# Turning tiles by 16-bit transposing transfers in place of TensorE transposes, in a streaming-encoder block

## The chip, the cores and the metric

The kernel runs on one core of a Trainium2 chip. The metric is the device time of one execution in microseconds, as the median of several runs. A profiled execution gives the trace from which single durations are read.

## The reference

One layer of a hybrid encoder block on 256 tokens of 2048 features, in float32. Norms are RMS norms with a gain, and every branch is added to the residual `x`:

```
x += 1/2 * SwiGLU(norm(x))                      # d_ff = 5632: h @ w_up, silu(gate) * up, @ w_down
h = norm(x); proj = h @ w_in                    # HGRN2 q f i g | RG-LRU x gate | branch gates A B
y_A = HGRN2(q, f, i) (normed, * silu(g))        # chunked gated linear recurrence
y_B = RG-LRU(conv4(x_b)) * gelu(gate_b)         # associative scan
merged = sigmoid(gate_A) * (y_A @ w_a) + sigmoid(gate_B) * (y_B @ w_b)
x += merged @ w_out
x += CrossAttention(norm(x), norm(mem))         # 4 heads, 256 memory tokens
x += 1/2 * SwiGLU(norm(x))
out = norm(x)
```

## The kernel before

**Products.** All large products are made at float32 precision from two float32r parts: a raw tile `raw` is copied to a high part `h` on ScalarE (`split`, L155), and VectorE writes the low part `l = raw - h` (L156). A product is then three matmuls: h by high, h by low, l by high. Weights come as 128x2048 tiles (1 MB). `weights()` keeps two weight tiles prepared ahead of TensorE; the tiles of the high parts come from a pool of three, `hp`, those of the low parts from a pool of three, `lp`. SyncE issues the loads, GpSimd the accumulating loads (L274, L313) and the transfers that prepare sums of weights ahead (L212, L218). The feed-forwards combine weight blocks so that seven products replace eight; the sums that this needs are VectorE's work (L304 to L307, and `ready` ones that were prepared and stored earlier).

**Stages.** First feed-forward, input projection with the two recurrences beside it, gates, the branch products (`ab`), the output product (`out`), cross-attention (`q`, `k`, `mv`, scores, `o`), second feed-forward. Each feed-forward runs over 11 groups of 512 hidden features: eight weight tiles of `w_up` per group, and after a group some blocks of `w_down` of earlier groups (`ffn_order`).

**Turns.** The residual `xt[c]` (four tiles of 512 features), the merged branches and the gated activations are kept by tokens, 128 tokens on the partitions. A product needs them by features. `turned` (L496) and `turn` in `ffn` (L607) do this with TensorE: eight transposes of 128x128 float32 for one tile of 128x1024, into two PSUM banks. From PSUM, ScalarE copies the high part (`Operands.add` L396, `add_two` L407, `hidop` L611, `operand_pairs` L520) and VectorE writes the low part (L397, L408, L612).

A tile is turned after the next weight blocks have been issued, by lists of delayed calls: `late` in the stages, whose `flush` runs everything in it after the high parts of a product, and `late` in `ffn`, where a call waits for a number of ticks, one tick a weight tile:

```
late.append((4 if g else 2, lambda g=g, hid=(e0, e3): turn(g, hid)))
```

The order within each engine is then made by a list scheduler that follows the order of the program as far as operands and buffers allow. Each engine works through its instructions in order, so an instruction that waits holds up those behind it.

Of the kernel before, what the change touches and what calls it, by code (L numbers as in the profile page):

```python
# [8 lines left out]
F32 = mybir.dt.float32  # L9
F32R = mybir.dt.float32r  # L10
ACT = mybir.ActivationFunctionType
ALU = mybir.AluOpType

P = 128
# [80 lines left out]
def block_kernel(ctx: ExitStack, tc: tile.TileContext, xT, xin, memT, vec, gfin, bgate, lruw, wu1, wd1, win, wv,  # L95
# [265 lines left out]

    def flush(late):
        while late:
            late.pop(0)()

    def summed(acc, out=None, by=None):
# [9 lines left out]
    class Operands:  # L376
# [13 lines left out]
        def add(self, src, gain=None):  # L390
            t = self.new()
            if gain is None:
                act.activation(t[:, :T], src, ACT.Copy)
                dve.tensor_tensor(out=t[:, T:], in0=src, in1=t[:, :T].bitcast(F32), op=ALU.subtract)
            else:
                act.activation(t[:, :T], src, ACT.Copy, scale=gain)  # L396
                dve.scalar_tensor_tensor(out=t[:, T:], in0=src, scalar=gain, in1=t[:, :T].bitcast(F32),  # L397
                                         op0=ALU.mult, op1=ALU.subtract)
# [91 lines left out]
    def turned(tile, which=range(2)):  # L490
# [22 lines left out]
    def operand_pairs(src, gain, q, xg, out, every=False):  # L513


        for a in src:
            i = len(out)
            g = xg[:, i * 512:(i + 1) * 512]
            for z in range(2):
                act.activation(g[:, z * T:][:, :T], a[:, z * T:(z + 1) * T], ACT.Copy,  # L520
                               scale=col(gain, 4 * q + 2 * i + z))
            h, l = slot(F32R, "xh"), slot(F32R, "xl")
# [59 lines left out]
    }  # L582

    def ffn(name, pairs, sq, then, begin=(), sums=()):

# [7 lines left out]
        hids, accs = {}, {}  # L593
        late = []
        rstd = None
# [6 lines left out]
        def turn(g, hid):  # L602
            for y in range(2):
# [7 lines left out]
                act.activation(ov[:, :, 0], av, ACT.Copy)  # L611
# [11 lines left out]
        for at, e in enumerate(order):  # L623
# [3 lines left out]
            if kind != "down":  # L627
# [13 lines left out]
                if ends or last:  # L641
                    if ends or kind == "plain":
# [3 lines left out]
                        else:  # L646
                            ev = scoped["wide"].tile([P, 2048], F32, name="ev", tag="wide")
                            e0, e1, e2, e3 = (ev[:, i * 512:(i + 1) * 512] for i in range(4))
                        if rstd is None:
# [6 lines left out]
                if last:  # L656
# [3 lines left out]
                    else:  # L660
# [119 lines left out]
    def to_mix(c, t):  # L780
# [295 lines left out]
    def merge(c, accs):  # L1076
# [8 lines left out]
        def turn():  # L1085
            for acc in turned(m):
                merged.add_two(acc)

        late.append(turn)

    accs = []
    for g in range(8):
        accs.append([bank(), bank()])
        for kq in range(2):
            rows_product(accs[-1], ys.tiles[8 * (g % 2):], weights("ab", g, kq), 4 * kq, kq == 0, kq == 1)
            flush(late)
        if g % 2:
# [9 lines left out]
    for c in range(4):  # L1107
        accs = [bank(), bank()]
        for kq in range(4):
            rows_product(accs, merged.tiles, weights("out", c, kq), 4 * kq, kq == 0, kq == 3)  # L1110
            flush(late)
# [88 lines left out]
    pairs2, sums2, sq4 = [], [], TokenSquares()  # L1200

    def to_ffn(c):
        out = []
        sums2.append(operand_pairs(turned(xt[c]), "ffn2_norm", c, slot(name="xg"), out, every=True))
        pairs2.extend(out)
# [14 lines left out]
    for c in range(4):  # L1220
        accs = [bank(), bank()]
        for kq in range(4):
            rows_product(accs, os.tiles, weights("o", c, kq), 4 * kq, kq == 0, kq == 3)
            flush(late)
# [125 lines left out]
```

## Time and profile before

| | |
|---|---|
| median of 3 runs | 2417.07 us (2416.99 to 2417.82) |
| the profiled execution | 2418.76 us, of which the span of the trace is 2417.0 us |
| TensorE busy | 2405.1 us |
| VectorE busy | 2044.6 us |
| ScalarE busy | 1468.6 us |
| GpSimd busy | 102.3 us |
| moved by DMA | 684.33 MB, 283 GB/s over the span |

The trace lists each instruction with its line, engine, tiles written and read, start and duration. PE is TensorE (PEld its weight loads), DVE VectorE, ACT ScalarE, POOL GpSimd, SP SyncE; a q behind the name is the engine's queue, which issues transfers. Matmuls are pipelined: the duration of one overlaps the next, so that the distance between two starts is the time for which one occupies the engine. Groups show `out<-in` with the tiles' names, a count, busy microseconds, the mean duration in nanoseconds, and the engine's idle time just before, with what ended it.

### The profile page before, as it was taken

To read this page: it belongs to the slowest core of one execution; us is meant where nothing else is said; L and a number is where in the kernel's file an instruction comes from. 1 tells how busy PE (TensorE), PEld (TensorE's weight loads), DVE (VectorE), ACT (ScalarE), POOL (GpSimd) and SP (SyncE) were. 2 spreads that over 40 slices of the span, in tenths; PEclk is the share of its full clock that TensorE was granted. 3 is DMA by queue.
4 is the path that set the end of the run, shared out by engine and by line. 5 is a ranking of instruction groups with operands and counts; after the bars stand their busy time and mean duration, and the time that the engine had idled before them with its cause. 6 is when DMAs were issued, how large, how long until landed. Compare 5 with 4: busy or idle time off the path is not lost.

```text
span 2417.0 us, 30834 instructions
## 1 busy us (share of the span) xinstructions
PE 2405.1 (100%) x12116; PEld 2006.3 (83%) x12116; DVE 2044.6 (85%) x2275; ACT 1468.6 (61%) x1499; POOL 102.3 (4%) x166
## 2 busy tenths in 40 slices
PE   9999999999999999999999999999999999999998
PEld 8888888888888888888888888888888788888887
DVE  6999999999866878678876787777789999999995
ACT  8566777777654454476434555545676666666664
POOL 0000000000000000000000000000000000000000
PEclk9999999999999999999999999999999999999999
DMA  8578999999858776878989899876788877787773
GB/s 305 203 227 258 276 277 278 273 275 271 270 215 318 276 285 240 302 269 324 353 323 348 291 358 344 324 286 244 265 344 308 292 283 279 269 287 279 285 282 140
DMA packets 102386, 684.33 MB, mean 283 GB/s; under 512 B 11360, under 2 KB 11616, under 8 KB 29280
## 3 DMA queue, kind: packets, MB, share of 16 engines
q1 hardware_dynamic: 78192, 518.68, 57.5%
q0 software_dynamic: 23328, 162.54, 22.4%
q8 instruction: 95, 1.56, 0.2%
q10 hardware_dynamic: 720, 1.13, 0.1%
q14 instruction: 51, 0.42, 0.0%
HBM read 619.39 MB, written 62.91 MB: 282 GB/s over the span
## 4 chain that ended last, share of the span: by engine, by line
PE 97%; DVE 1%; ACT 1%; DMA 1%; issue 0%; ACTq 0%
PE acc L566 18%; PE acc L567 18%; PE acc L569 18%; PE acc L332 11%; PE acc L357 8%; PE acc L358 8%; PE acc L360 8%; PE acc L335 6%; PE acc L607 1%; PE acc L496 1%; ACT h L155 1%; DVE l L156 0%; PE acc L904 0%; DMA raw<-wd 0%; PE acc L1197 0%; PE acc L1151 0%
## 5 line engine op out<-in xcount | busy, mean ns | idle before, releaser
L155 ACT ACTIVATE h<-raw 128x2048 fp32r<-128x2048 f32 (+3 forms) x578 | 867.6, 1526 | 618.8 <-PE acc L358 209.5
L156 DVE TENSOR_TENSOR l<-raw,h 128x2048 fp32r<-128x2048 f32 (+2 forms) x406 | 833.8, 2056 | 209.3 <-ACT h L155 206.3
L566 PE MATMUL acc<-h,xh 128*128 128x512 f32 x1228 | 478.4, 392 | 0.5 <-ACT h L155 0.5
L567 PE MATMUL acc<-h,xl 128*128 128x512 f32 x1228 | 476.1, 390 | 0.0
L357 PE MATMUL acc<-h,ops 128*128 128x512 f32 x832 | 326.8, 393 | 0.0
L358 PE MATMUL acc<-h,ops 128*128 128x512 f32 x832 | 324.6, 390 | 0.0
L332 PE MATMUL acc<-ops,h 128*128 128x512 f32 x1152 | 278.0, 393 | 0.0
L566 PE MATMUL acc<-h,hidop 128*128 128x512 f32 x704 | 276.3, 392 | 1.5 <-ACT h L155 1.5
L566 PEld LDWEIGHTS acc<-h,xh 128*128 128x128 f32 x1228 | 230.5, 188 | 54.4 <-ACT h L155 6.2
L567 PE MATMUL acc<-h,hidop 128*128 128x512 f32 x704 | 274.4, 390 | 0.0
L567 PEld LDWEIGHTS acc<-h,xl 128*128 128x128 f32 x1228 | 230.6, 188 | 46.7
L332 PEld LDWEIGHTS acc<-ops,h 128*128 128x128 f32 x1152 | 211.6, 188 | 41.6
L156 DVE TENSOR_TENSOR tl<-raw,h 128x1024 fp32r<-128x1024 f32 x172 | 203.7, 1220 | 13.8 <-ACT h L155 13.3
L360 PE MATMUL acc<-l,ops 128*128 128x512 f32 x832 | 205.8, 389 | 0.0
L155 ACT ACTIVATE h<-td 128x1024 fp32r<-128x1024 f32 x140 | 146.6, 1055 | 82.6 <-DVE td L304 31.5
L569 PE MATMUL acc<-l,hidop 128*128 128x512 f32 x704 | 190.5, 389 | 0.0
L360 PEld LDWEIGHTS acc<-l,ops 128*128 128x128 f32 x832 | 156.2, 188 | 32.4
L357 PEld LDWEIGHTS acc<-h,ops 128*128 128x128 f32 x832 | 156.2, 188 | 32.3
L358 PEld LDWEIGHTS acc<-h,ops 128*128 128x128 f32 x832 | 156.3, 188 | 31.5
L569 PE MATMUL acc<-tl,xh 128*128 128x512 f32 x624 | 178.1, 392 | 0.1
L156 DVE TENSOR_TENSOR tl<-td,h 128x1024 fp32r<-128x1024 f32 x140 | 170.1, 1220 | 8.3 <-ACT h L155 7.4
L569 PE MATMUL acc<-l,xh 128*128 128x512 f32 x604 | 166.5, 390 | 0.0
(245 smaller groups left out, 2750.5 us busy)
## 6 DMA issues: line engine op xcount, KB each, us to landing
raw<-wu SPq DMA_DIRECT2D x114, 1024.0 KB, 6.3
raw<-wd SPq DMA_DIRECT2D x88, 1024.0 KB, 6.5
prep<-wu POOLq DMA_DIRECT2D x58, 1024.0 KB, 6.5
t<-prep POOLq DMA_DIRECT2D x58, 1024.0 KB, 5.7
raw<-t SPq DMA_DIRECT2D x58, 1024.0 KB, 7.1
raw<-wu SPq DMA_DIRECT2D x58, 768.0 KB, 4.8
raw<-win SPq DMA_DIRECT2D x40, 1024.0 KB, 4.9
raw<-wg SPq DMA_DIRECT2D x32, 1024.0 KB, 5.1
```

The source lines that it names most:

```text
L155: done["high"] = act.activation(h, raw, ACT.Copy).ins
L156: done["low"] = dve.tensor_tensor(out=l, in0=raw, in1=h.bitcast(F32), op=ALU.subtract).ins
L332: pe.matmul(acc, h[:, k * P:(k + 1) * P], xs[k], start=k == 0, stop=False)
L335: done["product"] = pe.matmul(acc[:, :T], l[:, k * P:(k + 1) * P], xs[k][:, :T], start=False, stop=k == KT - 1).ins
L357: pe.matmul(accs[t], x[:, t * P:][:, :P], h[j], start=first and j == 0, stop=False)
L358: pe.matmul(accs[t], x[:, T + t * P:][:, :P], h[j], start=False, stop=False)
L360: done["product"] = pe.matmul(accs[t], x[:, t * P:][:, :P], l[j], start=False, stop=last and j == 3).ins
L496: pe.transpose(acc[:, z * T + t * P:][:, :P], tile[:, t * 512 + (2 * y + z) * P:][:, :P], ident)
L566: pe.matmul(acc, ah, bh, start=start, stop=False)
L567: pe.matmul(acc, al, bh, start=False, stop=False)
L569: pe.matmul(acc, ah, bl, start=False, stop=stop)
L607: pe.transpose(acc[:, z * T + t * P:][:, :P], hid[t][:, (2 * y + z) * P:][:, :P], ident)
```

## The change

Some turns are made by a transposing transfer of 16-bit elements. A float32 is seen as two halfwords. `planes` (ScalarE) copies a 128x1024 float32 tile as 2048 halfwords a partition and puts the 1024 low halfwords first and the 1024 high ones behind them. `across` issues from ScalarE's queue one transfer that transposes each 128x128 block of halfwords (sixteen blocks). `end_turn` and `turned_planes` (ScalarE) put the halfwords together again as float32, and the splits into high and low parts read this SBUF tile in place of PSUM.

It is done for:

- the second feed-forward's gated activations, all 11 groups, and the first feed-forward's last group (`BY_DMA`), with the copy back after six ticks
- the residual's tiles 0 and 1 ahead of the input projection (`mix_norm`), 0 to 2 ahead of cross-attention (`xattn_norm`), 0 and 1 ahead of the second feed-forward
- the merged branches' tiles 0 to 2

The other turns stay on TensorE. `flush` can take a number, and with `flush(late, 1)` one delayed call is made for each weight tile; some calls that do nothing put a turn one or two weight tiles later. The tile of the gated activations has its two halves side by side (`e0, e3, e1, e2`), and the other half of the pair serves as the planes.

```diff
+BY_DMA = {"ffn1": range(10, 11), "ffn2": range(0, 11)}
...
-    def flush(late):
-        while late:
+    def flush(late, n=1 << 30):
+        while late and n:
             late.pop(0)()
+            n -= 1
...
+        def add_pair(self, v):
+
+            self.new()
+            self.new()
+            ov = self.cur.rearrange("p (z s t n) -> p z s t n", z=2, s=2, t=2)
+            act.activation(ov[:, :, 0], v, ACT.Copy)
+            dve.tensor_tensor(out=ov[:, :, 1], in0=v, in1=ov[:, :, 0].bitcast(F32), op=ALU.subtract)
...
+    def planes(a, b):
+
+        act.activation(b.bitcast(U16).rearrange("p (two n) -> p two n", two=2),
+                       a.bitcast(U16).rearrange("p (n two) -> p two n", two=2), ACT.Copy)
+
+    def across(a, b):
+
+        act.dma_start_transpose(a.bitcast(U16).rearrange("p (i n) -> p i n", n=P), b.bitcast(U16))
+
+    def begin_turn(tile, free=False):
+
+        a = slot(name="planes")
+        b = tile if free else slot(name="across")
+        planes(tile, a)
+        across(b, a)
+        return b, a
+
+    def end_turn(b, a):
+
+        act.activation(a.bitcast(U16).rearrange("p (n two) -> p two n", two=2),
+                       b.bitcast(U16).rearrange("p (two n) -> p two n", two=2), ACT.Copy)
+        v = a.rearrange("p (t k n) -> p k t n", t=2, k=4)
+        return [v[:, k] for k in range(4)]
...
     def normed(ops, c, gain):
-        accs = turned(xt[c])
+        if gain in begun_turns:
+            parts = end_turn(*begun_turns.pop(gain))
+        else:
+            accs = turned(xt[c])
+            parts = [accs[m // 2][:, m % 2 * T:][:, :T].rearrange("p (t n) -> p t n", t=2) for m in range(4)]
         for m in range(4):
-            ops.add(accs[m // 2][:, m % 2 * T:][:, :T], col(gain, 4 * c + m))
+            ops.add(parts[m], col(gain, 4 * c + m))
...
+        def turned_planes(g, a, b):
+            act.activation(b.bitcast(U16).rearrange("p (n two) -> p two n", two=2),
+                           a.bitcast(U16).rearrange("p (two n) -> p two n", two=2), ACT.Copy)
+            bv = b.rearrange("p (t k n) -> p k t n", t=2, k=4)
+            for y in range(2):
+                o = slot(F32R, "hidop")
+                ov = o.rearrange("p (z s t n) -> p z s t n", z=2, s=2, t=2)
+                act.activation(ov[:, :, 0], bv[:, 2 * y:2 * y + 2], ACT.Copy)
+                dve.tensor_tensor(out=ov[:, :, 1], in0=bv[:, 2 * y:2 * y + 2], in1=ov[:, :, 0].bitcast(F32),
+                                  op=ALU.subtract)
+                hids[2 * g + y] = o
...
-                    late.append((4 if g else 2, lambda g=g, hid=(e0, e3): turn(g, hid)))
+                    if g in BY_DMA[name]:
+                        late.append((1, lambda ev=ev: planes(*ev)))
+                        late.append((1, lambda ev=ev: across(*ev)))
+                        late.append((6, lambda g=g, ev=ev: turned_planes(g, *ev)))
+                    else:
+                        late.append((4 if g else 2, lambda g=g, hid=(e0, e3): turn(g, hid)))
...
-        if c < 3:
+        if c in (0, 1):
+            going = begin_turn(xt[c])
+            def go(c=c, going=going):
+                begun_turns["mix_norm"] = going
+                normed(xs2, c, "mix_norm")
+            ffn_late.append((1, go))
+        elif c < 3:
             normed(xs2, c, "mix_norm")
...
+        if c in (0, 1, 2):
+            begun = begin_turn(m, True)
+            def turn():
+                parts = end_turn(*begun)
+                for y in range(2):
+                    merged.add_pair(begun[1].rearrange("p (t k n) -> p k t n", t=2, k=4)[:, 2 * y:2 * y + 2])
+            late.extend([lambda: None] * 1)
         late.append(turn)
...
-            flush(late)
+            flush(late, 1)
...
-        late.append(lambda c=c: normed(xs3, c, "xattn_norm"))
+        if c in (0, 1, 2):
+            going = begin_turn(xt[c])
+            def go(c=c, going=going):
+                begun_turns["xattn_norm"] = going
+                normed(xs3, c, "xattn_norm")
+            late += [lambda: None] * 1 + [go]
+        else:
+            late.append(lambda c=c: normed(xs3, c, "xattn_norm"))
...
+        if c in (0, 1):
+            turns4[c] = begin_turn(xt[c])
+            late += [lambda: None] * 2
         late += [lambda c=c: to_ffn(c)] if c < 3 else [lambda y=y: to_ffn_half(y) for y in range(2)]
```

In the changed kernel's numbering, the planes copy is L516, the transfer L521, the copies back L533 and L668, the splits L159 (ScalarE) and L160 (VectorE), and the transposes that stay on TensorE L511 and L659.

More of the change, by code (lines that the diff above doesn't have):

```diff
@@ L10 @@
 F32R = mybir.dt.float32r
+U16 = mybir.dt.uint16
 ACT = mybir.ActivationFunctionType
@@ L395, in add @@
             else:
-                act.activation(t[:, :T], src, ACT.Copy, scale=gain)
-                dve.scalar_tensor_tensor(out=t[:, T:], in0=src, scalar=gain, in1=t[:, :T].bitcast(F32),
+                tv = t.rearrange("p (s t n) -> p s t n", s=2, t=2) if len(src.shape) > 2 else t.rearrange(
+                    "p (s n) -> p s n", s=2)
+                act.activation(tv[:, 0], src, ACT.Copy, scale=gain)
+                dve.scalar_tensor_tensor(out=tv[:, 1], in0=src, scalar=gain, in1=tv[:, 0].bitcast(F32),
                                          op0=ALU.mult, op1=ALU.subtract)
@@ L519, in operand_pairs @@
             for z in range(2):
-                act.activation(g[:, z * T:][:, :T], a[:, z * T:(z + 1) * T], ACT.Copy,
-                               scale=col(gain, 4 * q + 2 * i + z))
+                if isinstance(a, list):
+                    act.activation(g[:, z * T:][:, :T].rearrange("p (t n) -> p t n", t=2), a[z], ACT.Copy,
+                                   scale=col(gain, 4 * q + 2 * i + z))
+                else:
+                    act.activation(g[:, z * T:][:, :T], a[:, z * T:(z + 1) * T], ACT.Copy,
+                                   scale=col(gain, 4 * q + 2 * i + z))
             h, l = slot(F32R, "xh"), slot(F32R, "xl")
@@ L593, in ffn @@
         hids, accs = {}, {}
-        late = []
+        late = ffn_late
+        late.clear()
         rstd = None
@@ L647, in ffn @@
                             ev = scoped["wide"].tile([P, 2048], F32, name="ev", tag="wide")
-                            e0, e1, e2, e3 = (ev[:, i * 512:(i + 1) * 512] for i in range(4))
+                            e0, e3, e1, e2 = (ev[:, i * 512:(i + 1) * 512] for i in range(4))
+                            ev = ev[:, :1024], ev[:, 1024:]
                         if rstd is None:
@@ L1200, in block_kernel @@
     pairs2, sums2, sq4 = [], [], TokenSquares()
+    turns4 = {}
     def to_ffn(c):
         out = []
-        sums2.append(operand_pairs(turned(xt[c]), "ffn2_norm", c, slot(name="xg"), out, every=True))
+        if c in turns4:
+            v = end_turn(*turns4.pop(c))
+            tiles = [v[:2], v[2:]]
+        else:
+            tiles = [[a[:, z * T:(z + 1) * T].rearrange("p (t n) -> p t n", t=2) for z in range(2)] for a in turned(xt[c])]
+        sums2.append(operand_pairs(tiles, "ffn2_norm", c, slot(name="xg"), out, every=True))
         pairs2.extend(out)
```

7 lines of the change are left out of this document (5 added, 2 removed).

## The prediction

> **What bounds the kernel now.** I read the page first: busy times, the slices, the chain of waits.
>
> ```profile
> span 2417.0 us, 30834 instructions
> PE 2405.1 (100%) x12116; PEld 2006.3 (83%) x12116; DVE 2044.6 (85%) x2275; ACT 1468.6 (61%) x1499; POOL 102.3 (4%) x166
> ...
> PEclk9999999999999999999999999999999999999999
> DMA  8578999999858776878989899876788877787773
> ...
> PE 97%; DVE 1%; ACT 1%; DMA 1%; issue 0%; ACTq 0%
> ```
>
> TensorE runs 2405.1 of 2417.0 us at the full granted clock, and 97% of the chain is its own matmuls. So time that leaves its instruction stream leaves the span, as long as what feeds it keeps up. DMA and VectorE are well loaded, ScalarE less. Next I cut the second feed-forward, where half the change lies, into windows:
>
> ```profile
> core 0: us, PE busy (x) PEld busy (x) DVE busy (x) ACT busy (x) POOL busy (x), PEclk, DMA share, GB/s
> ...
> 2050.00:2150.00 100.00, 100.00 (x450) 82.44 (x449) 91.67 (x85) 64.22 (x57) 0.87 (x1) 1.00 0.75 272
> ...
> sum 605.00, PE 602.92 PEld 495.41 DVE 558.40 ACT 401.04 POOL 6.94; mean PE 100.49 PEld 82.57 DVE 93.07 ACT 66.84 POOL 1.16
> ```
>
> In these 605 us TensorE idles 2.1 us. VectorE is at 92%, ScalarE at 66%: VectorE is the one close behind.
>
> **What leaves TensorE.** The order of instructions shows 176 matmuls fewer on TensorE, all transposes: 88 of the second feed-forward's 88 (L607, hid), 8 of the first's 88, 24 of 32 of the merged branches and 56 of 96 of the residual (L496). That is 22 turns of eight. What one turn costs is read from the starts in the timeline, since the durations overlap:
>
> ```profile
> 2113.68 0.62 PE L569 MATMUL acc<-l,hidop 128*128 128x512 f32 x2
> 2114.14 1.03 PE L607 MATMUL acc<-vt,hid 128*128 128x128 f32 x8
> 2114.93 0.48 PE L566 MATMUL acc<-h,hidop 128*128 128x512 f32 x1
> 2115.24 0.40 PE L567 MATMUL acc<-h,hidop 128*128 128x512 f32 x1
> 2115.48 0.39 PE L566 MATMUL acc<-h,hidop 128*128 128x512 f32 x1
> 2115.71 0.39 PE L567 MATMUL acc<-h,hidop 128*128 128x512 f32 x1
> ```
>
> Matmuls follow each other every 0.23 us. The eight transposes put 0.79 us between 2114.14 and 2114.93, and the matmul behind them takes 0.31 instead of 0.23: 0.87 us a turn. From above the cost is bounded by the busy time of the groups:
>
> ```profile
> L496 PE MATMUL acc<-vt,x 128*128 128x128 f32 x96 | 13.2, 274 | 0.0
> L607 PE MATMUL acc<-vt,hid 128*128 128x128 f32 x88 | 12.0, 272 | 0.0
> ```
>
> 12.0 us over 11 turns is 1.09, but the last transpose's 0.27 us run beside the next matmul, so I keep 0.87. **22 x 0.87 = 19.1 us**, of which 9.6 lie in the second feed-forward.
>
> The Trainium skill (TensorE: Matmul & The Clock Gate, Part 4: PE-mode transpose) gives a transpose of 128x128 about 275 ns in a kernel's context; 176 of those would be 48 us. The rows' 272 to 274 ns agree with it as a duration, but the starts 0.11 us apart show that TensorE is held for less than half of it, so the measurement decides and that sum has no chance.
>
> **What is added on ScalarE.** Each turn gets a copy that separates the 16-bit halves (planes, 2048 elements a partition), the issue of the transfer, and a copy back. The copies that split into high parts stay in number, and VectorE has as many instructions as before (the same operations, now reading SBUF). For a copy of 2048 elements:
>
> ```profile
> L282 ACT ACTIVATE h<-raw 128x2048 fp32r<-128x2048 f32 x18 | 34.3, 1906 | 1.9 <-DVE tl L156 1.3 <-PE acc L567 0.4
> ```
>
> 22 x 2 x 1.91 = 84 us, 11 x 3.8 = 42 of them in the second feed-forward: ScalarE there goes from 66% to 73%. A halfword copy is not in the trace; half as dear (0.95, half the bytes) or twice (3.8) are my ends, and the same element count makes me take 1.91 (three such copies stand in the tightest chain below: 6 us later at twice the price, 3 sooner at half). The share alone costs nothing. What counts is the place: ScalarE works in order, so the copy back, which waits for the transfer, holds up the weight splits (L155) behind it. One turn of the second feed-forward before:
>
> ```profile
> 2104.49 1.33 ACT L599 ACTIVATE hid<-hid,rtok 128x512 f32<-128x512 f32 x2
> 2108.04 1.49 ACT L155 ACTIVATE h<-raw 128x1536 fp32r<-128x1536 f32 x1 [2.22 <-issue]
> 2113.48 2.01 ACT L155 ACTIVATE h<-raw 128x1024 fp32r<-128x1024 f32 x2 [3.95 <-PE acc L567]
> 2115.39 1.07 ACT L611 ACTIVATE hidop<-acc 128x512 fp32r<-128x512 f32 x2
> 2119.81 1.49 ACT L155 ACTIVATE h<-raw 128x1536 fp32r<-128x1536 f32 x1 [3.35 <-issue]
> 2122.03 3.39 ACT L155 ACTIVATE h<-raw 128x1024 fp32r<-128x1024 f32 x3 [0.73 <-PE acc L567]
> ```
>
> In the new order the planes copy comes after the activation (2105.8 to 2107.7, in an idle gap of 2.2), the issue after the 1536 split (2109.5), the copy back after the two 1024 splits (2115.5), then the two hidop copies. So a transfer of up to 6.0 us is waited for by nobody. The copy back and the hidop copies then end at 2118.5, before the split at 2119.81: 7.3 us delay nothing. The issue itself can hold ScalarE's queue for 3 us without harm, since 3.95 us of idle time follow it. Beyond 7.3, the late splits eat their lead over TensorE:
>
> ```profile
> 2125.23 0.39 PE L566 MATMUL acc<-h,xh 128*128 128x512 f32 x1
> ...
> 2126.59 0.39 PE L566 MATMUL acc<-h,xh 128*128 128x512 f32 x1
> ```
>
> The block at 2125.23 uses the 1536 split, and its fourth product, at 2126.59, the first 1024 ones, which were done at 2124.0: 2.6 us of lead and 0.73 of idle time, so TensorE waits once a transfer takes over about 10.6 us, 1 us for each further one.
>
> **How long a transfer takes.** No transfer of this kind is in the trace. It moves half a megabyte; the nearest rows (KB, median us from issue to landing):
>
> ```profile
> l<-wd POOLq DMA_DIRECT2D x16, 1024.0 KB, 12.3
> ...
> bgate<-bgate SPq DMA_DIRECT2D x4, 512.0 KB, 6.1
> mem<-memT SPq DMA_DIRECT2D x4, 512.0 KB, 9.7
> lw<-lruw SPq DMA_DIRECT2D x2, 512.0 KB, 5.9
> ...
> out<-x ACTq DMA_DIRECT2D x4, 256.0 KB, 3.1
> ```
>
> Half-megabyte loads need 5.9 to 9.7 us behind other loads of their queue; ScalarE's queue is else empty, and 256 KB on it take 3.1 us. Twice that is 6.2, next to bgate and lw, and I take 6.5, with 3.1 below and 12.3 (the accumulating transfer, which isn't a plain one either) above. At 6.5 the second feed-forward gives its 9.6 us whole. VectorE's subtraction behind the hidop copies starts when they end, some 2 us later than before; the two x updates around it and its 8% of idle time take that up.
>
> On the DMA engines the volume is 22 x 0.52 = 11.5 MB on 684:
>
> ```profile
> q1 hardware_dynamic: 78192, 518.68, 57.5%
> ```
>
> 57.5% of 2417 us for 518.68 MB is 2.7 us of all 16 engines per MB, so a transfer is 1.4 us if it is as cheap as these. Four times that, 5.6 us, would raise the second feed-forward's share by 11 x 5.6 / 605 = 0.10; the slices of the first feed-forward run at nine tenths with TensorE full. I put 0 on it.
>
> **The middle turns.** Merged branches, cross-attention and the start of the second feed-forward have one 2048 split between issue and copy back. There a weight block is 24 matmuls of 0.23, 5.5 us, and uses one of three h tiles for 18 of them. A tile that is refilled when it comes free is needed again two blocks and 1.4 us later, less its own 1.9 us of writing: 10.4 us of lead. A wait of 6.5 minus what the split covers fits: 0. The tightest place is the end of the first feed-forward (`to_mix`, mix_norm), where both turns follow each other on ScalarE:
>
> ```profile
> 665.15 1.92 ACT L155 ACTIVATE h<-raw 128x2048 fp32r<-128x2048 f32 x1 [0.33 <-PE acc L567]
> ...
> 682.72 1.90 ACT L155 ACTIVATE h<-raw 128x2048 fp32r<-128x2048 f32 x1
> ```
>
> ```profile
> L458 ACT ACTIVATE junk<-x 128x512 f32<-128x512 f32 x40 | 25.1, 628 | 31.3 <-DVE x L681 27.8 <-DVE x L1104 3.1
> ...
> L396 ACT ACTIVATE ops<-acc,vt 128x256 fp32r<-128x256 f32 x32 | 14.2, 471 | 10.9 <-DVE ops L397 7.1 <-PE acc L496 3.6
> ...
> L476 ACT ACT_TABLE_LOAD x3 | 3.8, 1283 | 0.1
> ```
>
> From 667.1: transfer 6.5 (a square, waiting for the next residual chunk, lies in it), copy back 1.9, square 0.6, four gain copies 1.9, planes 1.9, split 1.9, transfer 6.5, copy back 1.9, two squares 1.3, four gain copies 1.9, and three more with a table load for the third turn, 2.7, reach 696; the split that stood at 682.72 is 13.5 us late against 10.4 of lead. I give back **3 us** here: 0 at 4 us a transfer, 14 at 12.
>
> **The sum.** 2418.76 (the profiled execution: 2417.0 and 1.8 around the span) - 19.1 + 3 = 2402.7. The median of the runs shown, 2417.07, is 1.7 lower than the profiled one: **2401.0**.
>
> **Rivals.** *A, the forecast*: 2397 to 2405.
>
> *B, VectorE keeps the second feed-forward's pace.* It is busy 558 of 605 us, and stands idle mostly for ScalarE (here over 1745 to 2400):
>
> ```profile
> DVE l L156 <- ACT h L155: 28.7, 24, 3.1
> ```
>
> If ScalarE's longer queue adds 9.6 us to these 28.7, TensorE gets none of the 9.6 us saved there: 2417.1 - 9.5 + 3 = 2410.6; half of it lost is 2405.8. For it: the 92%. Against: TensorE idles only 2.1 us there, and with 9.6 us less VectorE would still be at 94%.
>
> *C, slow transfers (the other side).* Place: the copy back (L668) on ScalarE. From 10.6 us on, each transfer of the second feed-forward costs TensorE its excess. At 10.6 mix_norm loses 11, and 13 us more for each further us, so it decides at about 11.2. At 12.3, the accumulating transfer's price, it is 11 x 1.7 = 19 and 15: 2417.1 - 19.1 + 34 = 2432. For it: that row, and data cut into halfwords; against: every plain row of this size is under 10.
>
> The Trainium skill (VectorE: DVE Perf Modes, The three transpose paths) speaks for C: 1309 ns for a 128x128 block by the crossbar, 390 by TensorE. Sixteen blocks one after another would be 20.9 us, an estimate, and by C's rule 11 x 10.3 = 113 us lost in that stage alone. This trace has 0.87 / 8 = 0.11 us a block on TensorE, so the 390 is not this stream's price, and no run so far shows the other figure.
>
> *D, nothing moves*: transfers near 11 us give back what is saved, 2412 to 2422. That the transposes stay on TensorE is ruled out by the order of its instructions.
>
> **Chances.** A 0.58, B 0.20, C 0.17, D 0.05. Within 0.2% (4.8 us), about what a measurement of this kernel can tell from no change, lies D alone. Faster 0.78, same 0.05, slower 0.17. The range takes A, B and half of D: 2395.9 (all 19.1 and the stage's 2.1 idle us gained, nothing given back) to 2417.
>
> **What would show it.** Right: 80 transposes left on L659 (the first feed-forward's) and 48 on L511; TensorE busy about 19 us less and still 99%; transfers (L521) landing within 4 to 8 us; ScalarE's wait at L668 under 2 us. Wrong: landings over 12 us and PE waiting for ACT L159 or DVE L160 after each group (C); VectorE's share at 95% and up with PE waiting for its l (B). A planes copy far from 1.9 us would break the ScalarE term.

## The result: 269 us slower

The changed kernel takes 2686.26 us (median of 4 runs, 2681.79 to 2697.67) against 2417.23 for the kernel before on the same chip: 1.112 times as long, 95% interval 1.1085 to 1.1155. The prediction was 2401.0 with a range up to 2417.0. The profiled execution took 2681.79 us. Where the runs of one kernel fall into a faster and a slower group over 1.5% apart, as they do in one experiment below, its ratio is taken of the faster ones.

The page of the changed kernel, with the lines that answer to those of before, and the rows of SyncE's and ScalarE's DMA queues (q1, q10) from its third part:

```profile
span 2680.0 us, 30519 instructions
PE 2438.7 (91%) x11940; PEld 2011.8 (75%) x11940; DVE 2042.2 (76%) x2275; ACT 1556.7 (58%) x1543; POOL 102.3 (4%) x166
...
PEclk9999999998999999997897999998999898989989
...
q1 hardware_dynamic: 78192, 518.68, 55.1%
...
q10 hardware_dynamic: 46480, 12.67, 5.7%
...
DMA 11%; PE 8%; DVE 7%; ACT 4%; issue 3%; DVEq 0%; ACTq 0%; SPq 0%
```

The 176 transposes are gone (11940 matmuls instead of 12116), and yet TensorE is busy for longer (2438.7 us for 2405.1) and idle for 241.3 us where it was idle for 11.9. The chain of waits, which the view here follows back only to 1816 us, through the last third of the span, has 11% of the span in transfers and 8% in TensorE. Before, TensorE had carried 97% of a chain that reached over the whole span.

What TensorE and ScalarE wait for, from the view of waits (total, times, longest, in us). `hid` and `hd` are the second feed-forward's gated activations, `ev` those of the first's last group, `across` the residual's tiles and `merge` the merged branches':

```profile
PE acc L361 <- ACT h L159: 94.4, 8, 32.5
PE acc L615 <- ACT h L159: 90.1, 24, 16.3
PE acc L615 <- ACT hidop L674: 22.3, 2, 19.6
```

```profile
ACT h L159 <- issue: 124.5, 22, 17.9
...
ACT hd L668 <- DMA hid<-hd: 74.8, 10, 16.6
ACT planes L533 <- DMA across<-planes: 53.4, 5, 25.3
ACT planes L533 <- DMA merge<-planes: 43.8, 3, 33.1
```

TensorE waits for ScalarE, 207 us in the three rows: for the weight splits (L159) and, twice, for the hidop copies behind a copy back. ScalarE stands still at two places of a turn: behind the issue of the transfer, and at the copy back (L668, L533), where it waits in order for the landing. The total of the row ended by issue isn't all behind transfers, since "issue" is idle time for which the profile shows no other cause, and the kernel before has such a row too, in short pieces:

```profile
ACT h L155 <- issue: 69.8, 26, 3.5
```

Worked out from the instructions of the trace, the 22 issues hold ScalarE's queue for 188.5 us in sum, and in 163.7 of them ScalarE does nothing. The view of the line that issues the transfers gives both (duration of the issue, smallest, median and largest in ns, then the landing):

```profile
L521 ACTq DMA_TRANSPOSE hid<-hd x11: 1912/9159/15643, 1919.6 to 2611.5; - x11
L521 ACTq DMA_TRANSPOSE across<-planes x7: 2962/5269/18392, 687.5 to 1816.4; - x7
L521 ACTq DMA_TRANSPOSE merge<-planes x3: 3145/13614/14810, 1216.4 to 1316.5; - x3
...
DMA to landing us min/median/max: 4.8/15.2/49.9
```

The turn of the second feed-forward with the longest issue and the latest landing of the eleven, on ScalarE, from the timeline (start, duration, and in brackets the idle time before and its cause), to be compared with the turn that the prediction shows:

```profile
2218.64 1.92 ACT L516 ACTIVATE hd<-hid 128x2048 uint16<-128x2048 uint16 x1 [1.47 <-DVE hid L652]
2220.46 1.48 ACT L159 ACTIVATE h<-raw 128x1536 fp32r<-128x1536 f32 x1
2220.59 15.64 ACTq L521 DMA_TRANSPOSE hid<-hd  x1
2236.36 2.00 ACT L159 ACTIVATE h<-raw 128x1024 fp32r<-128x1024 f32 x2 [14.42 <-issue]
2254.93 2.48 ACT L668 ACTIVATE hd<-hid 128x2048 uint16<-128x2048 uint16 x1 [16.57 <-DMA hid<-hd]
2257.44 1.15 ACT L674 ACTIVATE hidop<-hd 128x512 fp32r<-128x512 f32 x2
2258.50 2.41 ACT L159 ACTIVATE h<-raw 128x1536 fp32r<-128x1536 f32 x2
```

The issue keeps ScalarE's queue for 15.6 us; the two 1024 splits behind it start after 14.4 us of idle time. The transfer lands 34.3 us after its issue began (2254.91), and the copy back has waited 16.6 us for it. The split at 2258.50 is the one that TensorE needs next: in the same timeline its product stands at 2260.02 with 16.27 us of idle time before it.

Windows over one stage, merged branches and start of the cross-attention, show the rest (columns as in the prediction's windows; the last three are the granted clock, the busy share of the DMA engines and GB/s). First the kernel before, then the changed one:

```profile
1210.00:1330.00 120.00, 120.00 (x551) 99.80 (x550) 86.97 (x86) 52.08 (x48) 9.07 (x17) 1.00 0.90 333
```

```profile
1210.00:1330.00 120.00, 76.09 (x306) 61.48 (x305) 51.02 (x54) 39.19 (x25) 4.27 (x8) 0.80 0.83 201
```

The window has the same times in both traces, so in the changed kernel, 20 to some 70 us late by then, it covers somewhat earlier work. TensorE executes 306 matmuls where it executed 551. In the stretches in which it idles the granted clock is lower, 0.80 here, which stretches the matmuls that do run. And the DMA engines are nearly as busy as before (0.83 for 0.90) while they move 201 GB/s in place of 333.

Where the loss lies is read by the start of the same matmul (transposes not counted) in the two traces: the changed kernel is level up to 625 us, 21 us late at the end of the first feed-forward and the mixer's norm, 120 when the cross-attention's first product starts, 140 at the start of the second feed-forward, 263 at the end. So the second feed-forward with its 11 transfers loses 123, the 11 transfers ahead of it 140.

The trace also has a record of each DMA packet. By these, one of the 22 transfers, the one at 699 us, had almost no load beside it, a single packet of 2 KB or more; it landed in 4.8 us, the quickest of all.

### The profile page after: what moved, and what is told of

Same layout as the page of the kernel before. It is cut to its first block, busy times and chain, and to the rows that moved or that the text cites. A ratio compares the mean times of both kernels' runs of the same rounds, so it can differ in the third digit from the quotient of the medians.

```text
span 2680.0 us, 30519 instructions
## 1 busy us (share of the span) xinstructions
PE 2438.7 (91%) x11940; PEld 2011.8 (75%) x11940; DVE 2042.2 (76%) x2275; ACT 1556.7 (58%) x1543; POOL 102.3 (4%) x166
## 3 DMA queue, kind: packets, MB, share of 16 engines
q10 hardware_dynamic: 46480, 12.67, 5.7%
## 5 line engine op out<-in xcount | busy, mean ns | idle before, releaser
L159 ACT ACTIVATE h<-raw 128x2048 fp32r<-128x2048 f32 (+3 forms) x578 | 863.9, 1524 | 582.9 <-issue 124.5
L160 DVE TENSOR_TENSOR l<-raw,h 128x2048 fp32r<-128x2048 f32 (+2 forms) x406 | 832.6, 2055 | 293.6 <-ACT h L159 292.7
L615 PE MATMUL acc<-h,xh 128*128 128x512 f32 x1228 | 489.6, 401 | 90.0 <-ACT h L159 87.4
L616 PE MATMUL acc<-h,xl 128*128 128x512 f32 x1228 | 483.8, 396 | 0.0
L361 PE MATMUL acc<-h,ops 128*128 128x512 f32 x832 | 335.1, 403 | 94.4 <-ACT h L159 94.4
L362 PE MATMUL acc<-h,ops 128*128 128x512 f32 x832 | 331.8, 399 | 0.0
L615 PE MATMUL acc<-h,hidop 128*128 128x512 f32 x704 | 279.3, 397 | 25.1 <-ACT hidop L674 22.3
L616 PE MATMUL acc<-h,hidop 128*128 128x512 f32 x704 | 277.9, 395 | 0.2 <-DVE hidop L675 0.2
L361 PEld LDWEIGHTS acc<-h,ops 128*128 128x128 f32 x832 | 161.2, 194 | 131.9 <-ACT h L159 97.8
L160 DVE TENSOR_TENSOR tl<-raw,h 128x1024 fp32r<-128x1024 f32 x172 | 203.1, 1217 | 55.8 <-ACT h L159 55.7
L159 ACT ACTIVATE h<-td 128x1024 fp32r<-128x1024 f32 x140 | 146.6, 1055 | 82.3 <-DVE td L308 28.2
L362 PEld LDWEIGHTS acc<-h,ops 128*128 128x128 f32 x832 | 161.0, 193 | 33.1
L160 DVE TENSOR_TENSOR tl<-td,h 128x1024 fp32r<-128x1024 f32 x140 | 169.8, 1218 | 9.0 <-ACT h L159 8.1
L615 PEld LDWEIGHTS acc<-h,hidop 128*128 128x128 f32 x704 | 134.5, 191 | 55.7 <-ACT hidop L674 23.2
```

Source lines behind the costliest of these rows:

```text
L159: done["high"] = act.activation(h, raw, ACT.Copy).ins
L160: done["low"] = dve.tensor_tensor(out=l, in0=raw, in1=h.bitcast(F32), op=ALU.subtract).ins
L361: pe.matmul(accs[t], x[:, t * P:][:, :P], h[j], start=first and j == 0, stop=False)
L362: pe.matmul(accs[t], x[:, T + t * P:][:, :P], h[j], start=False, stop=False)
L615: pe.matmul(acc, ah, bh, start=start, stop=False)
L616: pe.matmul(acc, al, bh, start=False, stop=False)
```

## The experiments

Except where it is said, each is the changed kernel with the edit shown, timed in 3 rounds beside the kernel before, which took 2418.1 to 2418.2 us there. Delays are read as above, by the start of the same matmul.

**The transfer in the loads' own queue.**

```
-        act.dma_start_transpose(a.bitcast(U16)...., b.bitcast(U16))
+        sp.dma_start_transpose(a.bitcast(U16)...., b.bitcast(U16))
```

> The transposing transfers are issued from SyncE's queue, behind the weight loads, in place of ScalarE's; nothing else is changed. Theory 1 (a transposing transfer itself shares the 16 DMA engines badly with loads from any queue): landings stay at 10 to 35 us, and the time is 2600 us or more, since loads behind it on SyncE's queue are now held up too. Theory 2 (its 2048 packets of 256 bytes take turns with the 8 KB packets of the other queue, one for one): in one queue with the loads there are no turns to take, landings fall to 5 to 10 us and the time to 2400 to 2450. Theory 3 (what costs is ScalarE's queue held by the issue, 188 us in all): ScalarE is free of it, so the time falls by 100 us or more, whatever the landings.

Measured: 2456.96 us (2455.53 to 2464.45), ratio 1.0167 [1.0151, 1.0183]. Issues and landings, from the view of the line:

```profile
L521 SPq DMA_TRANSPOSE hid<-hd x11: 1697/4901/6817, 1794.9 to 2393.5; - x11
...
DMA to landing us min/median/max: 4.3/7.8/12.0
```

The same 22 transposing transfers land in 7.8 us in the median instead of 15.2, in 12.0 at most instead of 49.9, and 229 of the 269 us are gone. A transposing transfer need not land late, then: it does so in ScalarE's queue, beside the loads. The run does not tell the second theory from the third, since the landings and ScalarE's free queue both came as they say, and the time is 7 us above the second's range. What remains is some 40 us, with ScalarE still waiting 41.4 us at L668 and 41.5 at L533.

**No transfer.** `across` does nothing and the copy back reads the planes; the operands come out unturned.

> The transfers are left out; both halfword copies of each turn stay on ScalarE, and the operands come out unturned. Theories 1, 2 and 3 (all of the loss comes from the transfer, its issue or the wait for it): 2396 to 2404 us, that is before less 19 us of transposes, and TensorE busy 2386 us. Theory 4 (the two copies a turn, 1.9 and 2.5 us, and the new order on ScalarE cost by themselves): over 2417 us.

Measured: 2407.94 us (2407.45 to 2408.56), ratio 0.9957 [0.994, 0.9974]. Even with transfers that cost nothing the change would bring 10.2 us (of the 2418.11 beside it), not the 16 to 19 forecast, and less than this run was expected to. TensorE is busy for 2388.3 us.

**Neither the transfers nor the two copies.** The splits read the tiles as they stand, unturned.

```
     def planes(a, b):
-        act.activation(b.bitcast(U16)...., a.bitcast(U16)...., ACT.Copy)
+        pass
...  (the two copies back likewise)
```

> Neither the transfers nor the two copies of 16-bit halves: the operands are split from the tiles as they stand, unturned. The transposes are all that is gone from TensorE (176 instructions, 19.3 us by busy time). Theory that the 9 to 10 us missing from the run without transfers (2407.9, a gain of 9.3 instead of 19) are the copies on ScalarE: the time is 2397 to 2400 here. Rival, TensorE's busy time is not what the transposes cost, since other work bounds those stages: the time stays at 2405 to 2409 with the copies gone too.

Measured: 2402.80 us (2401.19 to 2408.36), ratio 0.9943 [0.9927, 0.996]; the span is 2399.4 us, 17.6 less than before:

```profile
PE 2385.3 (99%) x11940; PEld 1989.3 (83%) x11940; DVE 2042.1 (85%) x2275; ACT 1467.8 (61%) x1499; POOL 102.3 (4%) x166
```

So the transposes are worth 15.4 us by the medians (of 2418.16 beside it) and 17.6 by the profiled spans, near the 19.1 of the prediction. The copies on ScalarE take 5.1 us of it by the medians, 7.4 by the spans; the intervals of the two ratios overlap, so that this is likely and not certain. The median is 3 to 6 us above what was expected and 2 below the rival's range; none of its runs came down to 2400.

**A plain copy in the transfer's place**, the same half megabyte in rows of 4 KB, in ScalarE's queue, the operands unturned.

```
-        act.dma_start_transpose(a.bitcast(U16)...., b.bitcast(U16))
+        act.dma_start(a.bitcast(U16), b.bitcast(U16))
```

> Each transposing transfer is replaced by a plain copy of the same half megabyte between the same tiles from the same queue (4 KB a partition), so that the operands come out unturned. Theories 1 and 2: issue 0.4 us, landing 4 to 8 us, time 2397 to 2410. Theory 3 too, since the issue is short. If any half megabyte on ScalarE's queue lands late beside the loads (no theory of mine): landings over 10 us, over 2450.

**The plain copy in runs of 256 B**, as two transfers of every second block of 128 halfwords, in the same queue, unturned.

```
+        for j in range(2):
+            av, bv = (v.bitcast(U16).rearrange("p (i two n) -> p i two n", two=2, n=P)[:, :, j] for v in (a, b))
+            act.dma_start(av, bv)
```

> Each transposing transfer is replaced by two plain copies, each of every second block of 128 halfwords, so that the same half megabyte moves in the same 2048 runs of 256 bytes; operands come out unturned. Theory 2 (small packets taking turns with large ones): landings 10 to 35 us as with the transposing transfer, time 2550 to 2700. Theory 1 (it is the transposing that shares badly): landings 5 to 10 us, time 2397 to 2420.

Measured: 2425.30 us with 4 KB rows (2419.66 to 2436.16, ratio 1.0033 [1.0018, 1.0047]), 2539.98 with runs of 256 B (2530.53 to 2544.67, ratio 1.0499 [1.0472, 1.0526]). The rows of the DMA issues (KB, median us to landing), of the copy in large rows, the copy in runs of 256 B, and the changed kernel:

```profile
hid<-hd ACTq DMA_DIRECT2D x11, 512.0 KB, 8.3
```

```profile
hid<-hd ACTq DMA_DIRECT2D x22, 256.0 KB, 11.2
...
merge<-planes ACTq DMA_DIRECT2D x6, 256.0 KB, 13.8
```

```profile
hid<-hd ACTq DMA_TRANSPOSE x11, 13.9
...
merge<-planes ACTq DMA_TRANSPOSE x3, 23.9
```

The plain copy in large rows misses what was expected of it by 15 us, with landings of 2.9 to 10.8 us. The copy in runs of 256 B comes out 10 us below the range of the account of turns and 120 above the other's. It moves the same bytes as the first, in smaller pieces and two transfers for one; it lands later (11.2 and 13.8 for half the bytes each) and costs 115 us more. Its queue has 46480 packets, as many as the changed kernel's. Its waits on ScalarE and TensorE show what it has and what it lacks:

```profile
ACT h L159 <- issue: 23.7, 10, 3.2
...
ACT hd L670 <- DMA hid<-hd: 76.5, 10, 13.8
ACT planes L535 <- DMA across<-planes: 53.8, 5, 14.7
ACT planes L535 <- DMA merge<-planes: 31.2, 3, 13.5
```

```profile
PE acc L617 <- ACT h L159: 42.9, 24, 6.1
PE acc L361 <- ACT h L159: 21.5, 5, 6.6
PE acc L617 <- ACT hidop L676: 9.6, 2, 7.1
```

The waits for landings are nearly those of the changed kernel (161.5 us against 172.0). Those behind the issue are not: a plain issue holds the queue for 0.7 us, and ScalarE does nothing for 8.2 us beside its issues, against 163.7. TensorE then waits 74.0 us in these rows, against 206.8. So of the 146 us between this run and the changed kernel most goes with what only the transposing transfer has, probably its long issue above all; that the issue alone does it was not tried by itself. The packets differ too: by the trace's records one of 256 B takes 19 ns in the mean here and 53 in the changed kernel, and the loads' 8 KB packets 352 and 369.

**Runs of 256 B in the loads' queue**, `sp.dma_start(av, bv)` in the edit above.

> The plain copy in runs of 256 B of an earlier run (2540.0 us in ScalarE's queue, landing 8 to 14 us in the median, 22 at most; operands unturned), issued in SP's queue, where the loads are. Theory that small packets in a queue of their own take turns with the large packets of another: here they follow the loads in one queue and land in 7 to 9 us as the transposing transfers in SP's queue did, and the time is 2425 to 2445. Rival, runs of 256 B are slow wherever they are issued: landing stays at 11 us or more and the time is above 2500.

Measured: 2448.48 us (2446.41 to 2449.94), ratio 1.0125 [1.011, 1.014].

```profile
hid<-hd SPq DMA_DIRECT2D x22, 256.0 KB, 6.5
...
merge<-planes SPq DMA_DIRECT2D x6, 256.0 KB, 5.3
```

The same packets land in 6.5 and 5.3 us where they took 11.2 and 13.8, and 91.5 us are gone (the time is 3 us above what was expected, the landings are below it). So in these runs the small packets are late in ScalarE's queue and not in the loads' own. In the loads' queue the kernel still loses 28 us, all of it in the second feed-forward, where ScalarE waits 30.8 us at the copy back. The account that foresaw this has the queues take turns, packet by packet. The packet records bear out part of it: a packet of 256 B itself takes 19 ns in the mean in both runs, but between the first and the last of a turn's 2048 the DMA engines serve 292 packets of 2 KB and more (median; at most 765) when the small ones come from ScalarE's queue, and 35 (at most 168) when they stand among the loads. Turns of one for one, which would be up to 2048 large packets, are not what they show.

**The second feed-forward by TensorE again**: `BY_DMA = {..., "ffn2": range(0)}`; the other sites keep the transfers.

> The changed kernel with the second feed-forward's gated activations transposed by TensorE again; residual and merged branches stay with the transfers. If the loss of each site is its own, as the delay against the kernel before adds up matmul by matmul (139.8 us by the start of the second feed-forward, 123 us in it), the time is 2550 to 2562. If the feed-forward inherits late loads from the sites ahead of it (a queue behind), it still loses there and the time is above 2570; if its loss was partly the one of the sites ahead, seen later, below 2540 cannot come out of this curve.

Measured: 2557.53 us (2539.46 to 2570.54), ratio 1.057 [1.0517, 1.0623]. The delay is 152 us at the start of the second feed-forward and 152 at the end: with its turns back on TensorE that stage loses nothing, so what it lost was its own and not inherited from the sites ahead.

**The copy back later**, in groups 0 to 9 of the second feed-forward, by the trace 2 to 7 weight splits further back on ScalarE than in the changed kernel. The copy back in `end_turn` gets the same `with`, which by the trace leaves the other sites as they were:

```
-            act.activation(b...., a...., ACT.Copy)
+            with tc.issue_after(done["high"]) if g < 10 else ExitStack():
+                act.activation(b...., a...., ACT.Copy)
```

once with the issue from SP, once from ScalarE as in the changed kernel, and once with the plain copy in 4 KB rows (unturned).

> The transposing transfer issued from SP's queue, as in the run before with that edit alone (2457.0 us), and the copy back placed 3 to 8 more ScalarE copies later in groups 0 to 9 of the second feed-forward; at the other sites the order on ScalarE stays as it was, so the run is read in the second feed-forward. Theory A, what is left of the loss is ScalarE standing still in order for a landing: the 41.4 us that its second feed-forward copy back waited go to under 10, and the time falls by some 20 to 40 us, to 2415 to 2437. Theory B, what is left is the issue holding SP's queue and delaying the loads behind it: the waits for the landing may go, but TensorE then waits for loads instead and the time stays at 2450 to 2460.

> The changed kernel (transposing transfer in ScalarE's queue) with the same later copy back in groups 0 to 9 of the second feed-forward. Theory A, ScalarE standing still for the landing: 74.8 us of waits at that copy back go to under 20 and the 123 us that the second feed-forward lost fall to 40 to 60, the time to 2600 to 2625. Theory B, the issue itself holding ScalarE's queue (3 to 16 us for each transfer, 100 us in the second feed-forward): the landing's waits go but the loss stays at 90 us or more, the time at 2650 to 2690.

> A plain copy of the same half MB in place of the transposing transfer (its operands stay unturned), and the later copy back. Issue costs under 0.5 us here, so theory B has nothing to lose: both theories put it at 2408 to 2415, 10 to 17 us below the plain copy with the early copy back (2425.3) and level with the run without any transfer (2407.9). If it stays at 2420 to 2425, what the plain copy cost over no transfer was not ScalarE's wait for the landing.

Measured from SP: 2445.66 us (2438.08 to 2454.04), ratio 1.0118 [1.0087, 1.0148]. The wait at L670 for hid falls from 41.4 to 3.7 us, and the second feed-forward's loss from 21.6 to 9.6 us. From ScalarE: 2617.4 (2608.49 and 2626.22; two further runs took 2655.49 and 2669.53), ratio 1.0822 [1.0779, 1.0866]. The time lies in the range of the first account, 69 us below the changed kernel. The trace is of the run of 2655.49 us: there the wait falls from 74.8 to 45.7 us only and the loss in the stage from 123 to 79, while ScalarE does nothing for 116.6 of the 131.5 us of its issues. With the plain copy: 2420.67 (2414.99 to 2429.80), ratio 1.0011 [0.9999, 1.0024]; the wait at L670 falls from 20.6 to 4.5 us, but the time is only 4.6 us below that with the early copy back, with intervals that overlap, in the range that was to say that the landing's wait was not what this copy cost. So standing still for the landing is about half of what the second feed-forward loses from SP. From ScalarE it is 44 of 123 us by the trace and at most 69 of 123 by the time, if all of it was gained there. In neither is it all.

**Later at every site**, with the issue from SP: the merged branches and the residual wait two more weight groups (`[lambda: None] * 3` for `* 1`, and 3 for 1 in `ffn_late`). The mixer's operands then stand in another order, so that neither this kernel nor the next computes the reference.

> The run before that issued from SP and copied back later in the second feed-forward (2445.7 us, span 2441.0), with the copy back also later at the residual and merged branches: two more weight groups (about 8 us of TensorE) ahead of it. Theory A (ScalarE standing in order for a landing is what those sites lose): the 46.8 us that ScalarE waits for the landings there in that run fall below 10, the delay of TensorE against the kernel before at the start of the second feed-forward falls from 14.3 us to 0 to 3, and the time is 2425 to 2435. Theory B (the issue of 3 to 5 us each in SP's queue delays the loads behind it): the delay there stays at 10 or more and the time at 2440 to 2447.

Measured: 2441.05 us (2436.30 to 2444.11), ratio 1.0093 [1.0078, 1.0108]. The time and the delay at the start of the second feed-forward, 13.6 us, are those of the second account. But the edit took away little of its wait, 36.4 of 46.8 us stayed, since by the trace the copies back at these sites moved back by one weight split at most; so it does not separate the two accounts by itself. Two rows of the same stage say more, of the transposing transfers and of the 256-B copies, both from SP:

```profile
1210.00:1330.00 120.00, 114.51 (x497) 94.39 (x496) 84.04 (x85) 66.52 (x51) 8.01 (x15) 0.97 0.99 341
```

```profile
1210.00:1330.00 120.00, 120.00 (x535) 99.43 (x535) 89.16 (x89) 70.76 (x60) 9.06 (x17) 1.00 0.98 352
```

The DMA engines are full in both, 0.99 and 0.98 where before had 0.90. ScalarE waits 41.5 us for landings at L533 in the first and 29.1 at the same copy in the second, yet in the second TensorE loses nothing: its delay at the start of the second feed-forward is 0.0 us, in the first 15.1. What differs beside the waits is SP's queue, held for 3.6 us in the median by a transposing issue and for 0.64 by each plain one, with the loads behind it. In the merged branches, at 0.9 busy, that is where the loss of the SP version most likely comes from.

**GpSimd makes the copies** (`nc.gpsimd.tensor_copy` in the three places of the run just told):

> As the run above, with both copies of 16-bit halves made by GpSimd in place of ScalarE. Theory that the copies on ScalarE cost what the transfers leave over (the run without any transfer gained 9 of the 19 us of the transposes): the time falls 5 to 15 us below the run above, to 2410 to 2425, if GpSimd makes one copy in up to 6 us. Rival: GpSimd is slower at these copies (10 us and more each) and its copies get in VectorE's way; the operands come late and the time is 2440 or above.

Measured: 2449.31 us (2440.49 to 2459.59), ratio 1.0117 [1.0094, 1.0141].

```profile
PE 2409.1 (98%) x11940; PEld 1992.8 (81%) x11940; DVE 2084.0 (85%) x2275; ACT 1468.1 (60%) x1499; POOL 240.0 (10%) x210
...
L516 POOL COPY hd<-hid 128x2048 uint16<-128x2048 uint16 x11 | 41.0, 3731 | 185.2 <-DVE hid L653 185.2
```

ScalarE is rid of its 90 us, but the copies take 2.4 to 4.0 us (means by site) instead of 1.9 to 2.5, VectorE's busy time rises by 40 us for the same instructions, and the median time by 8, with intervals that overlap. The outcome is the rival's, with copies less slow than it said.

No run that computes the reference beats the kernel before. The best single site, the end of the first feed-forward and the mixer's norm in the run with everything later, is 1.8 us ahead of it, less than a measurement can tell, and in a kernel that doesn't compute the reference.

## Why the prediction was wrong

The prediction asked for 16 us less and got 269 more, because the transfers landed two to four times as late as their 6.5 us and because their issue, which had no price, stopped ScalarE as well. Medians, each line one step from the one above (the kernel before took 2417.2 us beside the changed kernel and 2418.2 beside the next line):

| kernel | us | step |
|---|---|---|
| before | 2418.2 | |
| transposes left out, nothing put in their place | 2402.8 | -15.4 |
| with the copies of halves on ScalarE | 2407.9 | +5.1 |
| with a plain transfer in 4 KB rows, ScalarE's queue | 2425.3 | +17.4 |
| in runs of 256 B | 2540.0 | +114.7 |
| transposing (the change) | 2686.3 | +146.3 |

*TensorE, 19.1 us: right.* In time the transposes are worth 15 to 18 us. 11940 matmuls instead of 12116; 2385.3 us of busy time without stalls is 19.8 below the 2405.1 of before. The trace kept 80 transposes at L659 and 48 at L511, as foreseen.

*The copies, 1.91 us each: half right.* The copy into planes is 1.90 to 1.91 us, the copy back more:

```profile
L516 ACT ACTIVATE hd<-hid 128x2048 uint16<-128x2048 uint16 x11 | 21.0, 1908 | 9.7 <-DVE hid L652 9.6
...
L668 ACT ACTIVATE hd<-hid 128x2048 uint16<-128x2048 uint16 x11 | 27.5, 2500 | 74.8 <-DMA hid<-hd 74.8
```

The sum is 91 us on ScalarE (1558.9 of the run without transfers less 1467.8 of that without the copies too), not 84. The prediction gave this no price on the path; it costs some 5 to 7 us, as far as the overlapping intervals tell.

*The transfer, 6.5 us with ends 3.1 and 12.3: the step that failed.* The rows next to it were transfers in large rows, and a plain copy of that kind in ScalarE's queue did land in 8.3 us, not far off. The prediction noted that the data were cut into halfwords and then sized the transfer by bytes alone. The changed kernel's land in 13.9 us (hid) to 23.9 (merge) in the median and 49.9 at most, and the same transfers in the loads' queue in 7.8. So the term that was mis-sized is the transfer in a queue of its own beside the loads.

*The issue, "3 us without harm": failed.* It holds ScalarE's queue for 9.2 us in the median for hid and for up to 18.4 (a residual tile), and the splits behind it with it. The prediction had a row for the idle time that could take it up, but none for the issue itself, and no upper end.

*Nothing for the DMA engines: failed.* The share of q1 rises from 57.5% of 2417.0 us to 60.5% of 2453.7 when SP issues the transfers: 94.7 us of all 16 engines, 4.3 for each transfer, not 1.4. By the packet records the packets of 256 B alone are 3.6 us a transfer there and 6.8 in the changed kernel, where a plain copy in the same runs is 2.4. In the merged branches the SP version's 0.99 leaves almost nothing of the engines.

*mix_norm, 3 us back: the wrong place.* 21 us were lost at this end of the first feed-forward, but in the turn of ev just ahead, whose copy back waited 20.4 us for its transfer; across mix_norm the delay stayed at 21.

*TensorE at full clock throughout: failed.* For 11940 matmuls its busy time is 2438.7 us with stalls and 2385.3 in the run with neither transfers nor copies: 53 of the 281 us between those spans are longer busy time of the same matmuls, in windows whose granted clock is 0.80 to 0.96, the other 227 idle time. The prediction priced a wait of TensorE at its length alone.

*Rivals.* C was the right mechanism at the right place: ScalarE in order, the copy back, then late splits. Its size was wrong. Its rule, 1 us for each beyond 10.6, would need 22.7 us for each transfer to lose what the second feed-forward lost: 123 and the 9.6 saved, over 11, is 12.1. The eleven landings, 6.6 to 34.3 us by the trace, come to 96 us by that rule, of the 133 that were lost. The rule counted the landing, but the issue holds the same queue as well. B did not come: VectorE's share fell to 76%. Without transfers the second feed-forward gained 6.0 of its 9.6 us by the delays, and in that whole run TensorE waited 4.4 us for ScalarE's splits and 0.8 for VectorE's low parts.

The Trainium skill (VectorE: DVE Perf Modes, The three transpose paths), with 1309 ns for a block by the crossbar, led the prediction to an estimate of 113 us for that stage; the measured loss is 123. The agreement is by chance: a transfer of 16 blocks landed in 4.2 us where it was quickest (in the run with everything later), 0.26 us a block, so the blocks do not take 1309 ns each, one after another, here. The Trainium skill (Advanced Engine Details and Errata, X-Bar Transpose (TRN2)) holds such transfers to be as fast as regular ones; in the landing the runs come near it for SP's queue, with 8.0 us for hid against 8.3 for the plain copy in 4 KB rows in ScalarE's and 6.5 for each half in runs of 256 B in SP's, and disagree for ScalarE's own queue beside the loads, with 13.9 to 23.9.

Open: why a transposing issue holds its queue for 2 to 18 us where the two plain ones of together as many packets take 0.7 each; how the 146 us divide between that hold and the longer packets; and what the remaining 10 us are that the second feed-forward loses with the issue from SP and the late copy back, where TensorE's waits come in pieces of at most 1.7 us.

## What to carry to other kernels

Size a transfer by its packets and by the queue that it shares, not by its bytes alone: here the same 256-B pieces cost 91.5 us less in the queue of the large loads than beside it. Before an in-order engine is made to issue a transfer or to wait for one, list what stands behind it in its queue, and give the issue itself a price with an upper end. Where the bounding engine will idle, ask what the clock does: here 53 us of slower matmuls came on top of 227 us of idle time.

## What had not been expected of the hardware

- A transposing transfer of half a megabyte holds its issuing queue for 1.9 to 18.4 us (ScalarE's) or 1.7 to 9.9 us (SP's); a plain one for 0.47 us in 4 KB rows.
- In ScalarE's queue beside the loads a packet of 256 B of a transposing transfer takes 53 ns in the mean (up to 109 over one transfer), in the loads' queue 28, of a plain copy 19 in either.
- In the window shown, beside transposing transfers in a queue of their own, the DMA engines were 83% busy at 201 GB/s, where they had moved 333 GB/s at 90%.
- GpSimd copies of 128x2048 halfwords take 2.4 to 4.0 us, and VectorE's instructions became 2% longer beside them (2084.0 us for 2043.7).
